# Matmul prices in a kernel's ordering model: from nominal values to the spacings of the trace

## Chip, cores, metric

The kernel runs on one core of one Trainium2 chip. The metric is the device time of one launch in microseconds (us); of three runs the median counts. A core has five engines that work side by side: PE (TensorE, matmuls), DVE (VectorE), ACT (ScalarE), POOL (GpSimd) and SP (SyncE, which here issues the DMAs). Each engine takes its instructions strictly in the order in which the program holds them, and waits at an instruction whose inputs are not there yet.

## What is computed

A sequence of 256 tokens of width 1024 goes through four layers, in fp32. Only what the text speaks of is shown:

```python
# layer 0, even: stick-breaking attention beside an S5 state-space mixer
h = rms_norm(x, even_norm_g[0]);  proj = h @ even_w_in[0]
q, k, v, z_a, u, z_b = split(proj)          # 1024 1024 1024 1024 512 512
q = rms_norm(q per head);  k = rms_norm(k per head)      # 8 heads of 128
o_a = stick_breaking_attention(q, k, v) * silu(z_a)
o_b = s5_mixer(u, ...) * silu(z_b)          # 32 groups, 64 complex states each
x = x + concat(o_a, o_b) @ even_w_out[0]
# layer 1, odd: gated linear attention, chunks of 64, 4 heads
q, k, v, z, r = split(rms_norm(x) @ odd_w_in[0])
log_a = log_sigmoid(r @ w_gate + b_gate) / 16
x = x + (rms_norm(gla(q, k, v, log_a)) * silu(z)) @ odd_w_out[0]
# layers 2 and 3, hybrid: dilated window attention beside retention
for l in range(2):
    h = rmsnorm(x) * (1 + scale) + shift    # from c @ w_ada
    y_att, y_ret = attention(h @ w_in), retention(h @ w_in)
    x = x + gate * ((sig(ga) * (y_att @ w_pa) + sig(gr) * (y_ret @ w_pr)) @ w_out)
return rmsnorm(x, final_norm_w)
# s5_mixer: lam_bar = exp(lam*dt); b_bar = (lam_bar-1)/lam * b
# state_t = lam_bar * state_(t-1) + b_bar u_t ; y = gelu(Re(c state) + d u); y * sigmoid(y @ w_glu + b)
```

## The kernel before

**The weights.** All large products are made of three fp32r matmuls. A weight tile of 128x2048 comes by DMA into `raw`; ACT copies it into `whi` (the high part, fp32r, 1024 columns at a time), DVE subtracts to make `wlo` (the low part, 512 columns at a time), and the product is whi·Hhi + whi·Hlo + wlo·Hhi, with H the normed activations, split alike. There are three slots each for `raw`, `whi` and `wlo`. `proj_a` writes tokens by 512 columns (PSUM tile `pa`, matmuls of 512 columns), `proj_b` writes 128 columns by 256 tokens (`pb`, 256 columns). `plan` fixes the order of the weight tiles: for the even layer q of the first four heads, u, k, v of the first half, q, k, v of the second half, then the gates and the output; then the odd and the hybrid layers.

**Beside the projections** the even layer has these steps, all named by their tiles. `qraw` is q or k of one half; its mean squares go through a chain of some ten small DVE steps (`rs`, Newton for 1/sqrt), DVE scales `qraw`, PE transposes it four heads at a time (`qtp`), and DVE writes qT or kT. There are four such sets: q and k of each half ("q0", "k0", "q1", "k1"). `stick_fiber` then makes the scores (`sbz`) of a half and its attention (`sb_sp`). The S5 mixer has one preparation on DVE (`s5_prep`: a long row of small steps, `s_w`, that ends in the table `s_W`, then a sign step on `s_W`, then `s_L` alike), and four blocks of states (0 to 3). In a block POOL makes the table `s5ez` from `s_W` (products into `s5ez` and `s5t`, then their sum), PE transposes it (`s5ep`), ACT copies it (`s5E`), PE multiplies with u (`s5vp`), ACT copies (`s5V`), PE rotates (`s5jp`), DVE combines (`s5B`, `s5m`, a scan over time, `s5V`), PE rotates again (`s5jp`), POOL and DVE multiply (`s5m`), and PE gives the block's output (`s5yp`), with POOL's `s5F`, `s5f` and PE's `s5gp`, `s5tp` as further tables. `s5ez`, `s5F`, `s5m`, `s5f` have one or few slots, so a block's tables wait for the block before. In the odd layer `la` (DVE) is the logarithm of the decay, PE sums it over time (`lgt`), and `gkt`, `gsc`, `gst` are the steps of the linear attention.

**What sets the order.** Nothing of the order is written by hand. Each layer is a set of generators ("fibers") that yield instructions; `Engine.make` gives each instruction a price (`i.cost`), and `run` keeps a clock for every engine: of all the fibers' next instructions it takes the one that could start first by these clocks (`when`, which adds a latency between engines; some fibers have a bias on it), emits it and advances its engine's clock by the price (`issue`). So the program of each engine is in the order in which the model thought that the instructions could start, and the prices of matmuls say how many projection matmuls the model puts on PE while another engine works at something. For a matmul with fp32r operands of n columns the price is 0.4167 n + 2.5 ns: 215.9 ns for the 512 columns of `pa`, 109.2 ns for the 256 of `pb`. Fp32 matmuls cost 1.667 n + 10 ns and at least 214 ns, a transpose 107 ns. Line 275 (`i.eng, i.emit = ...`) is the place where every instruction is recorded, so all rows of the trace carry L275, and the tiles' names tell them apart.

Of the kernel before, what the change touches and what calls it, by code (L numbers as in the profile page):

```python
# [8 lines left out]
F32 = mybir.dt.float32  # L9
# [7 lines left out]
P = 128  # L17
T = 256
# [9 lines left out]
# Newton's steps for a scaled 1/sqrt: s' = -2 s^3 takes the scale of the first guess to 32  # L28
# [6 lines left out]
# ---------------------------------------------------------------- weight order  # L35
def plan():
# [30 lines left out]
    # the ada tiles, spread between the others  # L67
# [26 lines left out]
# misc: 0:64 position numbers, 64:128 zero at position 0 and one after it  # L94
# [142 lines left out]
# ---------------------------------------------------------------- the program  # L237
# Each layer is written as fibers, generators of instructions. The instructions of all fibers are put in
# one order by a model of the engines: next comes the one that could start first.
# [21 lines left out]
class Engine:  # L261
    """Makes instructions; they are issued when their turn comes."""
# [4 lines left out]
    def __getattr__(self, op):  # L267
        real, name = getattr(self.real, op), self.name

        def make(*a, **k):  # L270
# [5 lines left out]
            # a tile of PSUM serves one engine at a time  # L276
# [11 lines left out]
            elif name == "pe":  # L288
                rhs = a[2] if len(a) > 2 else k["rhs"]
                if op == "transpose":  # L290
                    i.cost = 0.107
                else:
                    n = _cols(rhs)
                    i.cost = (0.4167 * n + 2.5) * 1e-3 if rhs.dtype == F32R else max(0.214, (1.667 * n + 10) * 1e-3)
# [19 lines left out]
class Prog:  # L314
    """What the layers share: engines, slots of memory, the weight stream, the fibers and their order."""
# [17 lines left out]
    # ---- fibers  # L333
# [12 lines left out]
    def stop(self, f, tl):  # L346
        """Ends a fiber and gives back its tile."""
        f["live"] = False
        self.fibers.remove(f)
        self.put(tl)  # L350
# [8 lines left out]
    def when(self, i):  # L359
        """When an instruction could start."""  # L360
# [72 lines left out]
    # ---- slots  # L433
# [42 lines left out]
    # ---- the weight stream: load, then the high and the low part of every tile  # L476
# [51 lines left out]
    def slack(self):  # L528
        """How far the weights are ahead of their use, in tiles."""
        return (self.made - self.used) / 2048.0  # L530
# [11 lines left out]
    # ---- shift, scale and gate: sums of weighted rows over the partitions' share, then over partitions  # L542
# [56 lines left out]
    # ---- projections  # L599
    def proj_a(self, h, blocks, steps, evac, ready=None, bias=0.0, halves=()):  # L600
        """Token-major [token, 512], activations stationary: blocks of keys; steps: (block, key, token tile).

        The blocks in halves come out as two halves, the first one early."""
# [27 lines left out]
    def proj_b(self, h, key, evac, nk=8, c0=0, last=True, ready=None):  # L631
        """Feature-major, two blocks of 128 features: weights stationary, 256 tokens move."""
# [17 lines left out]
    def copy_out(self, dst):  # L650
        """An evacuation by a copy."""
# [5 lines left out]
    # ---- small arithmetic  # L657
# [17 lines left out]
    def silu2(self, zp, g):  # L675
        """2 silu(z) of a PSUM tile, which is given back."""
# [5 lines left out]
    # ---- norm of the residual  # L682
    def square(self, tt, c, w=512, on_dve=False):
        """Adds the sum of squares of some columns to a token tile's."""
# [17 lines left out]
    def norm_rstd(self, tt):  # L702
        """1/sqrt of a token tile's mean square and EPS."""
# [14 lines left out]
    def norm(self, tt, scale, bias=None, flags=()):  # L718
        """The norm of a token tile, transposed, as high and low parts."""
# [67 lines left out]
    def h_end(self):  # L787
        """After a layer's last product with the norm."""
# [4 lines left out]
    def out_proj(self, mix, ready, blocks, nxt, res_gate=None, halves=()):  # L793
        """x += mix @ w_out. nxt(tt): the generator that goes on with a finished token tile."""
# [26 lines left out]
        # the first token tile is done as early as three tiles of weights let it  # L821
# [26 lines left out]
def program(g):  # L848
# [7 lines left out]
    # ---- loads  # L856
# [33 lines left out]
    # the tables of the first functions, and the array's clock, before the first data come  # L890
# [29 lines left out]
def reduce_angle(g, r, ang, k):  # L920
    """r = ang less the nearest multiple of two pi, within [-pi, pi]."""
# [24 lines left out]
def s5_prep(g, ev, S):  # L946
    """Tables of the S5 mixer that hang on its parameters alone."""
# [1043 lines left out]
```

## Time and profile before

| | |
|---|---|
| median of three runs | 1058.98 us (1058.54 to 1060.42) |
| profiled execution, its span | 1059.9 us |
| PE busy | 1031.7 us, 97% of the span, 7058 matmuls |
| DVE, ACT, POOL busy | 757.2, 502.3, 64.2 us |
| HBM | 189.31 MB read, 180 GB/s over the span |

The page gives the span of one execution and nothing around it. Busy time of PE includes the time in which several matmuls overlap in its pipeline, so the spacing of starts, not the length of one matmul, is what a matmul costs in a row of them; the chain of waits shows this spacing, since it lists a row of matmuls with its length from the first start to the last. The granted clock is the share of full TensorE speed that the chip allowed; its two levels are 1.0 (2.4 GHz) and 0.5 (1.2 GHz), and a stretch with a value between them had both.

### The profile page before, as it was taken

To read this page: it belongs to the slowest core of one execution; us is meant where nothing else is said; L and a number is where in the kernel's file an instruction comes from. 1 tells how busy PE (TensorE), PEld (TensorE's weight loads), DVE (VectorE), ACT (ScalarE), POOL (GpSimd) and SP (SyncE) were. 2 spreads that over 40 slices of the span, in tenths; PEclk is the share of its full clock that TensorE was granted. 3 is DMA by queue.
4 is the path that set the end of the run, shared out by engine and by line. 5 is a ranking of instruction groups with operands and counts; after the bars stand their busy time and mean duration, and the time that the engine had idled before them with its cause. 6 is when DMAs were issued, how large, how long until landed. Compare 5 with 4: busy or idle time off the path is not lost.

```text
span 1059.9 us, 17583 instructions
## 1 busy us (share of the span) xinstructions
PE 1031.7 (97%) x7058; PEld 948.3 (89%) x7058; DVE 757.2 (71%) x1607; ACT 502.3 (47%) x756; POOL 64.2 (6%) x79
## 2 busy tenths in 40 slices
PE   8989979999999999999999999999999999999997
PEld 7967769978899789999899999978999989999995
DVE  6996675968889776766588967674565658984565
ACT  6647427646634654434422443455453442343442
POOL 0146340000110000000000000000000000000000
PEclk9989899999999999999999999999999999999999
DMA  8641124463864658564444567445645444454541
GB/s 293 209 161 64 51 80 140 151 212 129 308 240 174 250 213 305 205 231 148 159 160 159 199 241 267 168 143 215 237 161 199 173 166 159 139 181 167 198 173 40
DMA packets 33501, 192.53 MB, mean 182 GB/s; under 512 B 8171, under 2 KB 9195, under 8 KB 11148
## 3 DMA queue, kind: packets, MB, share of 16 engines
q1 hardware_dynamic: 33132, 190.90, 50.6%
q8 instruction: 55, 0.90, 0.3%
q10 hardware_dynamic: 288, 0.52, 0.1%
q14 instruction: 26, 0.21, 0.1%
HBM read 189.31 MB, written 1.05 MB: 180 GB/s over the span
## 4 chain that ended last, share of the span: by engine, by line
PE 88%; DVE 8%; issue 1%; ACT 1%; DMA 1%; POOL 1%; SPq 0%; DVEq 0%; ACTq 0%
PE pb L275 52%; PE pa L275 21%; PE as L275 4%; DVE wlo L275 2%; PE ret L275 2%; DVE rs L275 2%; PE sbz L275 1%; DVE s_w L275 1%; PE s5yp L275 1%; PE ntp L275 1%; PE s5vp L275 1%; DMA cols<-in_cols_dram 1%; PE gsc L275 1%; PE qtp L275 1%; DVE s5B L275 1%
## 5 line engine op out<-in xcount | busy, mean ns | idle before, releaser
L275 DVE TENSOR_TENSOR wlo<-raw,whi 128x512 fp32r<-128x512 f32 x604 | 394.4, 693 | 166.0 <-ACT whi L275 161.2
L275 PE MATMUL pb<-H,whi 128*128 128x256 f32 x2688 | 494.6, 285 | 0.0
L275 ACT ACTIVATE whi<-raw 128x1024 fp32r<-128x1024 f32 x302 | 307.4, 1053 | 314.9 <-issue 161.6
L275 PEld LDWEIGHTS pb<-H,whi 128*128 128x128 f32 x2688 | 420.8, 192 | 3.0 <-issue 2.0
L275 PE MATMUL pb<-H,wlo 128*128 128x256 f32 x1344 | 382.6, 285 | 0.0
L275 PEld LDWEIGHTS pb<-H,wlo 128*128 128x128 f32 x1344 | 257.6, 192 | 0.5 <-issue 0.2
L275 PE MATMUL pa<-whi,H 128*128 128x512 f32 x576 | 187.4, 401 | 2.9 <-DVE H L275 2.9
L275 PEld LDWEIGHTS pa<-whi,H 128*128 128x128 f32 x576 | 109.2, 191 | 28.3 <-DVE H L275 5.2
L275 PE MATMUL pa<-wlo,H 128*128 128x512 f32 x288 | 114.7, 398 | 0.0
L275 PE MATMUL pb<-yy,whi 128*128 128x256 f32 x384 | 69.5, 283 | 0.0
L275 PEld LDWEIGHTS pa<-wlo,H 128*128 128x128 f32 x288 | 54.9, 191 | 11.3 <-issue 0.7
L275 DVE SCALAR_TENSOR_TENSOR acc<-raw,cact,acc 128x512 f32<-128x512 f32 x84 | 59.1, 745 | 4.4 <-DMA raw<-in_wall_dram 4.2
L275 PEld LDWEIGHTS pb<-yy,whi 128*128 128x128 f32 x384 | 59.9, 192 | 0.0
L275 PE MATMUL pb<-yy,wlo 128*128 128x256 f32 x192 | 54.3, 283 | 0.0
L275 PE MATMUL pa<-whi,mg 128*128 128x512 f32 (+1 forms) x144 | 41.1, 368 | 0.0
L275 PEld LDWEIGHTS pb<-yy,wlo 128*128 128x128 f32 x192 | 36.9, 192 | 0.0
L275 PEld LDWEIGHTS pa<-whi,mg 128*128 128x128 f32 x144 | 26.0, 188 | 5.1
L275 PE MATMUL pa<-whi,mix 128*128 128x512 f32 x96 | 30.2, 393 | 0.3 <-ACT mix L275 0.3
L275 DVE SCALAR_TENSOR_TENSOR rs<-rs 128x1 f32<-128x1 f32 (+3 forms) x144 | 28.5, 198 | 2.7
L275 DVE SCALAR_TENSOR_TENSOR tg<-tg,pb 128x512 f32<-128x512 f32 x16 | 11.0, 688 | 26.4 <-PE pb L275 26.4
L275 ACT ACTIVATE sqj<-x 128x512 f32<-128x512 f32 (+1 forms) x19 | 11.5, 608 | 35.7 <-DVE x L275 33.5
L275 PE MATMUL pa<-wlo,mg 128*128 128x512 f32 (+1 forms) x72 | 26.9, 374 | 0.0
(277 smaller groups left out, 1082.1 us busy)
## 6 DMA issues: line engine op xcount, KB each, us to landing
raw<-in_wall_dram SPq DMA_DIRECT2D x174, 1024.0 KB, 4.9
x<-in_x_dram SPq DMA_DIRECT2D x2, 512.0 KB, 5.9
raw<-in_wall_dram SPq DMA_DIRECT2D x2, 512.0 KB, 7.0
s5bc<-in_s5bc_dram SPq DMA_DIRECT2D x4, 256.0 KB, 2.5
gate<-in_bgate_dram SPq DMA_DIRECT2D x2, 512.0 KB, 5.6
c<-in_cst_dram SPq DMA_DIRECT2D x1, 896.0 KB, 7.1
cst<-in_cst_dram SPq DMA_DIRECT2D x1, 704.0 KB, 12.0
s_room<-s_room SPq DMA_DIRECT2D x16, 32.0 KB, 3.4
```

The lines of the kernel that those rows point to most:

```text
L275: i.eng, i.emit = name, (lambda: real(*a, **k))
```

## The change

The prices of PE's instructions are replaced by others: a transpose 112 ns for 107; an fp32r matmul 0.4167 n + 13.4 ns for 0.4167 n + 2.5 (512 columns: 226.8 for 215.9; 256 columns: 120.1 for 109.2); an fp32 matmul 1.667 n + 4 ns, at least 224, for 1.667 n + 10, at least 214. The prices of the other engines, the latencies and the biases stay. The other pieces of the diff take out comments and docstrings.

```diff
@@ -288,10 +288,10 @@
             elif name == "pe":
                 rhs = a[2] if len(a) > 2 else k["rhs"]
                 if op == "transpose":
-                    i.cost = 0.107
+                    i.cost = 0.112
                 else:
                     n = _cols(rhs)
-                    i.cost = (0.4167 * n + 2.5) * 1e-3 if rhs.dtype == F32R else max(0.214, (1.667 * n + 10) * 1e-3)
+                    i.cost = (0.4167 * n + 13.4) * 1e-3 if rhs.dtype == F32R else max(0.224, (1.667 * n + 4) * 1e-3)
             else:
```

The instructions are the same, in another order on every engine. Three places follow; a row is one instruction, or as many as its x says, with its tiles and its shape.

DVE, the end of the preparation of the S5 table `s_W`, before; `s_w` and `s_W` are its small steps, `wlo` the low parts of weights, `rs` the norm of k0:

```order
L275 TENSOR_TENSOR s_W<-s_w 128x32 x2
L275 TENSOR_TENSOR s_w<-s_W,s_w 128x32 x3
L275 TENSOR_TENSOR wlo<-raw,whi 128x512 x2
L275 TENSOR_TENSOR s_w<-s_W,s_w 128x32
L275 TENSOR_TENSOR wlo<-raw,whi 128x512 x2
L275 TENSOR_TENSOR s_W<-s_w 128x32
L275 TENSOR_TENSOR wlo<-raw,whi 128x512 x2
L275 TENSOR_TENSOR s_W<-s_w 128x32
L275 TENSOR_TENSOR s_w<-s_W,s_w 128x32
L275 TENSOR_SCALAR rs<-qss 128x8
```

The same place after, up to the sign step (the row with `sgc`) and the rows behind it:

```order
L275 TENSOR_TENSOR s_W<-s_w 128x32 x2
L275 TENSOR_TENSOR s_w<-s_W,s_w 128x32 x4
L275 TENSOR_TENSOR s_W<-s_w 128x32 x2
L275 TENSOR_TENSOR s_w<-s_W,s_w 128x32 x4
L275 TENSOR_TENSOR s_W<-s_w 128x32
L275 TENSOR_TENSOR wlo<-raw,whi 128x512
L275 TENSOR_TENSOR s_W<-s_w 128x32
L275 TENSOR_TENSOR wlo<-raw,whi 128x512
L275 TENSOR_SCALAR s_W<-s_W,sgc 128x128
L275 TENSOR_TENSOR wlo<-raw,whi 128x512 x2
L275 TENSOR_TENSOR s_w<-s_L,s_w 128x32
L275 TENSOR_TENSOR wlo<-raw,whi 128x512
```

Counted over the whole program up to the sign step, five `wlo` and five `rs` steps that stood ahead of it stand behind it now.

PE, from the transposes of block 0's table on, before; `qtp` are the transposes of k0:

```order
L275 MATMUL pa<-wlo,H 128x512
L275 MATMUL pa<-whi,H 128x512
L275 MATMUL s5ep<-cst_76,s5ez 128x128 x4
L275 MATMUL pa<-whi,H 128x512
L275 MATMUL pa<-wlo,H 128x512
L275 MATMUL pa<-whi,H 128x512
L275 MATMUL qtp<-cst_76,qraw 128x128 x4
L275 MATMUL pa<-whi,H 128x512
L275 MATMUL pa<-wlo,H 128x512
L275 MATMUL pa<-whi,H 128x512 x2
L275 MATMUL pa<-wlo,H 128x512
L275 MATMUL pa<-whi,H 128x512
```

And after:

```order
L275 MATMUL s5ep<-cst_76,s5ez 128x128 x4
L275 MATMUL pa<-whi,H 128x512
L275 MATMUL pa<-wlo,H 128x512
L275 MATMUL pa<-whi,H 128x512 x2
L275 MATMUL s5gp<-s5f_159,s5ez 128x32 x3
L275 MATMUL s5vp<-s_room,s5E 128x64 x8
L275 MATMUL s5gp<-s5f_159,s5ez 128x32
L275 MATMUL pa<-wlo,H 128x512
L275 MATMUL pa<-whi,H 128x512 x2
L275 MATMUL s5jp<-s5V,cst_103 128x512
L275 MATMUL s5tp<-s5f_159,cst_103 128x8x16 x3
L275 MATMUL s5tp<-s5f_159,cst_76 128x8x16
```

In after 213 projection matmuls stand ahead of this `s5ep`, in before 240, and k0's `qtp` comes 12 `pa` and most of block 0's PE steps behind it, where it came 3 `pa` behind. Projection matmuls ahead of the end of the blocks' `s5yp`: 273, 318, 347, 369 before (blocks 0 to 3), 239, 273, 309, 330 after. The `sbz` of the first half (12 products of qT and kT) stand before block 0's `s5yp` in before, behind it in after; the `qtp` of q1 ahead of and behind block 1's `s5yp` in before, behind block 2's in after; the `qtp` of k1 between block 3's `s5ep` and `s5vp` in before, 37 `pa` behind block 3's `s5yp` in after.

POOL, around the end of block 0, before (`s5F` is block 0's table, the rows from `s5f` on are block 1's, except `s5m`, which is block 0's):

```order
L275 TENSOR_TENSOR s5F<-s5F,s5t 128x512
L275 MEMSET s5B 128x8
L275 TENSOR_SCALAR s5f_920<-s5bc,sgc 128x128
L275 TENSOR_TENSOR s5ez<-s_W,s5bc 128x16x16 x2
L275 TENSOR_TENSOR s5t<-s_W,s5bc 128x16x16 x2
L275 TENSOR_TENSOR s5m<-s_room,s5B 128x512
L275 TENSOR_TENSOR s5ez<-s5ez,s5t 128x512
```

And after:

```order
L275 MEMSET s5B 128x8
L275 TENSOR_TENSOR s5F<-s5F,s5t 128x512
L275 TENSOR_TENSOR s5m<-s_room,s5B 128x512
L275 TENSOR_SCALAR s5f_820<-s5bc,sgc 128x128
L275 TENSOR_TENSOR s5ez<-s_W,s5bc 128x16x16 x2
L275 TENSOR_TENSOR s5t<-s_W,s5bc 128x16x16 x2
L275 TENSOR_TENSOR s5ez<-s5ez,s5t 128x512
```

Block 0's `s5m` now stands ahead of block 1's tables. On SP a few loads of weight tiles change places with those of the S5 tables and with copies of the S5 output. In the odd layer `lgt` stands 20 `pb` earlier on PE; in the hybrid layers the steps beside the projections move by at most eight or so projection matmuls, and the ends of the layers move by eight matmuls at most.

## Rows read from the trace of the kernel before

**Rows 1.** the page: busy time by engine; granted clock in 40 slices.
```profile
PE 1031.7 (97%) x7058; PEld 948.3 (89%) x7058; DVE 757.2 (71%) x1607; ACT 502.3 (47%) x756; POOL 64.2 (6%) x79
...
PEclk9989899999999999999999999999999999999999
```

**Rows 2.** windows: length, busy PE PEld DVE ACT POOL, granted clock, DMA, GB/s.
```profile
50.00:100.00 50.00, 44.20 (x231) 35.28 (x230) 41.40 (x116) 31.30 (x56) 24.05 (x25) 0.90 0.39 128
100.00:150.00 50.00, 42.72 (x240) 34.07 (x239) 35.70 (x62) 22.41 (x55) 25.15 (x29) 0.90 0.19 63
...
450.00:500.00 50.00, 50.00 (x398) 48.96 (x397) 30.38 (x61) 21.72 (x33) 0.00 (x0) 1.00 0.57 204
...
700.00:750.00 50.00, 48.26 (x244) 39.74 (x243) 32.21 (x71) 30.58 (x48) 0.00 (x0) 1.00 0.51 176
```

**Rows 3.** chain of waits, 490 to 530: start, length, what.
```profile
498.98 21.79 PE pa L275 x96
```

**Rows 4.** the same view, 945 to the end.
```profile
950.74 78.71 PE pb L275 x656
```

**Rows 5.** PE in order of time: start, length, what, [idle before, its releaser].
```profile
62.46 0.66 PE L275 MATMUL s5ep<-cst,s5ez 128*128 128x128 f32 x4 [0.99 <-POOL s5ez L275]
...
67.45 1.09 PE L275 MATMUL qtp<-cst,qraw 128*128 128x128 f32 x4 [3.63 <-DVE qraw L275]
...
87.14 0.41 PE L275 MATMUL s5yp<-s_room,s5T 128*128 128x64 f32 x2 [1.13 <-DVE s5m L275]
...
115.02 0.66 PE L275 MATMUL qtp<-cst,qraw 128*128 128x128 f32 x4 [1.89 <-DVE qraw L275]
...
137.02 0.41 PE L275 MATMUL s5yp<-s_room,s5T 128*128 128x64 f32 x2 [1.87 <-DVE s5m L275]
...
144.18 1.11 PE L275 MATMUL qtp<-cst,qraw 128*128 128x128 f32 x4 [3.27 <-DVE qraw L275]
```

**Rows 6.** windows, the stretch around the longest of those waits.
```profile
65.30:72.10 6.80, 4.65 (x15) 3.97 (x16) 5.89 (x10) 0.00 (x0) 6.72 (x5) 0.50 0.52 164
```

**Rows 7.** windows from s5ep of block 0 on, cut behind each block's s5yp.
```profile
62.46:89.87 27.41, 22.60 (x129) 17.96 (x129) 21.71 (x45) 14.32 (x27) 16.57 (x15) 0.86 0.35 125
89.87:120.12 30.25, 28.36 (x151) 22.18 (x150) 21.46 (x43) 20.05 (x44) 11.60 (x14) 0.89 0.23 79
120.12:139.50 19.38, 17.26 (x99) 13.63 (x97) 13.04 (x18) 8.29 (x18) 13.50 (x14) 0.92 0.16 47
139.50:159.16 19.66, 16.17 (x99) 12.75 (x95) 13.12 (x22) 3.44 (x6) 5.44 (x7) 0.91 0.22 76
```

**Rows 8.** DVE in order of time.
```profile
52.72 1.29 DVE L275 TENSOR_TENSOR wlo<-raw,whi 128x512 fp32r<-128x512 f32 x2
...
55.34 1.29 DVE L275 TENSOR_TENSOR wlo<-raw,whi 128x512 fp32r<-128x512 f32 x2
...
58.30 0.64 DVE L275 TENSOR_TENSOR rs<-rs 128x8 f32<-128x8 f32 x1
58.86 0.72 DVE L275 TENSOR_SCALAR s_W<-s_W,sgc 128x128 f32<-128x128 f32 x1
...
66.63 1.28 DVE L275 TENSOR_TENSOR qraw<-qraw,rs 128x512 f32<-128x512 f32 x2
```

**Rows 9.** POOL in order of time.
```profile
59.73 1.31 POOL L275 TENSOR_TENSOR s5t<-s_W,s5bc 128x256 f32<-128x256 f32 x2 [0.23 <-DVE s_W L275]
61.12 1.28 POOL L275 TENSOR_TENSOR s5ez<-s5ez,s5t 128x512 f32<-128x512 f32 x1
...
131.95 2.09 POOL L275 TENSOR_TENSOR s5t<-s_W,s5bc 128x256 f32<-128x256 f32 x2
...
135.69 1.72 POOL L275 TENSOR_TENSOR s5ez<-s5ez,s5t 128x512 f32<-128x512 f32 x1
```

**Rows 10.** tile lgt: count, durations min/median/max, first and last start.
```profile
L275 PE MATMUL lgt<-cst,la x16: 270/275/275, 284.2 to 285.8; 128*128 128x128 f32 x16
...
L275 DVE SCALAR_TENSOR_TENSOR la<-lgt,la x1: 1217/1217/1217, 281.8 to 281.8; 128x1024 f32<-128x1024 f32 x1
```

## The prediction

> **What bounds the kernel now.** I read first the page's busy times, then the windows of 50 us, then the chain of waits, and last PE's own row of instructions where the windows show holes. PE is busy for 1031.7 of 1059.9 us, and the granted clock is full but for a few slices of the first sixth [rows 1]. The windows say where the rest is: from 450 to 500 us PE has no hole at all and the full clock, from 700 to 750 it lacks 1.74 us, but from 50 to 100 it lacks 5.80 us and from 100 to 150 7.28 us, both at a mean clock of 0.90 [rows 2]. So the kernel is bound by the stream of matmuls nearly everywhere, and by the small chains of DVE, POOL and ACT in the even layer, where PE runs out of things that it may do. A reordering takes no matmul away; it can win only holes and half-clock time, and nearly all of these lie between 50 and 160 us.
>
> The chain also shows what a matmul costs in a row: 96 `pa` in 21.79 us, 227 ns each [rows 3], and 656 `pb` in 78.71 us, 120 ns each [rows 4]. The new prices (226.8 and 120.1) are these; the old ones (215.9 and 109.2) were 5 and 9% too low, so the model believed PE early with its projections and put more of them ahead of a step than there was time for. The order of before therefore had some cover built in by mistake: a PE that arrives later than the model thinks. What happens when that goes is the question.
>
> Of the holes, six hold 12.8 us [rows 5]: 0.99 us at block 0's `s5ep` (POOL's `s5ez`), 3.63 at k0's transposes, 1.13 at block 0's `s5yp`, 1.89 at q1's transposes, 1.87 at block 2's `s5yp`, 3.27 at k1's transposes. The clock falls with them: around the longest the grant is 0.50, the lower level of 1.2 GHz, for 6.8 us [rows 6]. I cut the stretch behind each block's `s5yp` [rows 7] and split its loss into holes (length less PE busy) and clock ((1 - mean grant) x length, which is what half-speed time costs if PE had work all along):
> - block 0, 27.41 us: holes 4.81, clock 3.84
> - block 1, 30.25 us: holes 1.89, clock 3.33
> - block 2, 19.38 us: holes 2.12, clock 1.55
> - block 3, 19.66 us: holes 3.49, clock 1.77
>
> Together 22.8 us: the ceiling of what the order could win here.
>
> **The change part by part.** I hold each step of the new order against the point at which it would cost nothing: its old time, less the PE work that now stands behind it instead of ahead.
>
> *Block 0's start.* 27 projection matmuls fewer stand ahead of `s5ep`: 27 x 0.227 = 6.13 us, so it breaks even at 62.46 - 6.13 = 56.33. It waits for POOL's `s5ez`, and that for the sign step on `s_W`, which ended at 58.86 + 0.72 = 59.58 [rows 8]; POOL then needed until 61.12 + 1.28 = 62.40, 2.82 us [rows 9]. Five `wlo` less ahead of the sign step save 5 x 0.65 = 3.2 us (1.29 for two), and of the five `rs` steps the one at 58.30 alone 0.56 to the next start [rows 8]; the other four are too short to count. The sign step then ends at 55.8, `s5ez` at 58.6, and `s5ep` starts near 58.65: **+2.3 us** against break-even. The low end is 0, if DVE comes to the sign step another 2.3 us earlier than counted; the high end comes from company. In before only small steps ran on DVE while POOL made this table, in after the `wlo` that were pushed back. Where DVE was dense with `wlo` (block 3's table), the same two POOL steps took 2.09 and 1.72 us instead of 1.31 and 1.28 [rows 9]: 1.2 us more, so +3.5.
>
> The Trainium skill speaks against the change here: "SBUF — State Buffer", section "SBUF: two separate sides", says that DVE and GpSimd share a port pair as an exclusive lock, that a DVE step with two SBUF inputs contends with a GpSimd step that reads SBUF, and that the loser waits for the whole instruction. `wlo` has two SBUF inputs. The rows of block 3 agree with it (2.09 against 1.31); by this rule the high end would be the likely one.
>
> *Block 0 to its `s5yp`.* The hole at k0's transposes does not go. Behind the sign step DVE now has six `wlo` ahead of `qraw` instead of two (+2.6 us), the five `rs` steps and some five steps of S5 (about 0.65 each, as a `wlo`, an estimate: 3.3). It took 66.63 - 59.58 = 7.05 us before [rows 8]; about 13.5 now, from 55.8 to 69.3, and 0.8 for the first half of the scaling, as before (66.63 to 67.45) [rows 5, 8]: 70.1. PE is there at 58.65 + 12 x 0.227 + the S5 steps (about 4.9, an estimate from the lengths that PE spent on them) = 66.3. The hole is 3.8, as before 3.63. What goes is the 1.13 at `s5yp`: block 0's `s5m` stood behind three of POOL's steps for block 1's tables, now ahead of them. **-1.1 us**, with 0 and -8.6 (all of the block's loss) as ends; I stay near 0 because the large hole stays, and the half clock with it.
>
> *Block 1.* q1's transposes move from around block 1's `s5yp` to behind block 2's, some 9.8 us of PE work later, so the hole of 1.89 is not on the way any more; half of the slow clock (1.7) goes with it, the other half belongs to the holes of block 0. **-3.6 us** (0 to -5.2).
>
> *Block 2.* The wait of `s5yp` for `s5m` stays: the number of projection matmuls between is about the same (21 between `s5jp` steps and `s5yp`, before and after), and DVE now has q1's `rs` steps among its own. Half of the clock's loss goes with block 1's hole: **-0.8 us** (+1.5, eight `rs` steps of about 0.2 us more ahead of `s5m`, to -3.7).
>
> *Block 3.* k1's transposes, whose hole was the 3.27, move behind `s5yp` and 37 further `pa` (8.4 us of cover, where DVE still has some 8 `wlo`, 5 us, and the `rs` chain to do); half of the clock's loss goes with it: 3.27 + 0.9 = **-4.2 us** (0, if the hole appears at the new place, to -5.3). The work that moved behind block 3's `s5yp` (39 `pa` and eight transposes, 39 x 0.227 + about 0.9 = 9.7 us) is covered there: behind it PE has only projections.
>
> *The odd layer.* The second row of `lgt` started at 284.2, 1.2 us after `la` ended at 281.8 + 1.217 = 283.0 [rows 10]. It stands 20 `pb` earlier, 20 x 0.120 = 2.4 us, and DVE's share does not move by itself: 2.4 - 1.2 = **+1.2 us**, up to +3 if the following steps (`gkt`, `gsc`, 2 us earlier too) wait again, 0 if DVE's `wlo` ahead of `la` are fewer.
>
> *The rest.* In the hybrid layers the steps move by a microsecond of PE work or less, where PE now has no hole [rows 2]; the holes at the ends of the layers (1.74 us around 708) have the same chain before and after. 0 (-1 to +2). The DMAs move on SP, but HBM is at 180 GB/s, and POOL's and SP's other rows are not late anywhere that PE waits. 0.
>
> Sum: 2.3 - 1.1 - 3.6 - 0.8 - 4.2 + 1.2 = **-6.2 us**. On the profiled execution's 1059.9 that is 1053.7. This execution lies 0.9 us above the median of the runs, so on the scale of the runs 1052.8. I say **1053**.
>
> **The rivals.**
>
> *The holes only change place.* A chain of DVE, POOL and ACT that lasts as long as before makes PE wait for it somewhere: what q1's transposes no longer wait, `s5yp` waits a little later, since each block's products wait for the same `s5m`. For this speaks that all six holes end with DVE or POOL and that these two have the same work to do; against it that PE's work between the blocks is unchanged while DVE is dense only in parts. Then only k1's 4.2 us are real: 2.3 + 1.2 - 4.2 = -0.7, **1058**, no difference that a measurement of this kernel could tell (about 0.2%, 2.1 us).
>
> *Slower: the lost cover.* The too low prices gave each S5 step of PE more projections ahead than the model counted, and these hid the chains' real latencies. In after PE comes 6.1 us earlier to block 0's table and 9.7 us earlier to block 3's output than to the same steps in before, the chains do not get shorter, and POOL and DVE meet at the `wlo` that were pushed back. With no hole won back in blocks 0 to 3, the table late by the 1.2 us of company, and the odd layer as above: 2.3 + 1.2 + 1.2 = +4.7, and another 1.5 where block 2's `s5m` waits behind `rs`: **1064 to 1065**. It decides from where less than 4.7 of the 22.8 us, a fifth, is won back. The rule of the port pair belongs to this case.
>
> *Faster by much.* Two thirds of the blocks' loss goes: -15 + 3.5 = -11.5, **1047**. The holes and the half clock hang together, so one that vanishes takes 1 to 3 us of slow clock along.
>
> That the order does not change is out: the programs differ on every engine.
>
> **How the numbers follow.** The forecast (1049 to 1057) has 0.42, much faster (below 1049) 0.16, holes moved (1057 to 1061) 0.22, lost cover (above 1061) 0.20. The range of 8 in 10 runs from 1046.5 to 1062.5. Faster by over 0.2% (below 1056.9) is the first two, 0.58; within 0.2% 0.21; slower 0.21.
>
> **What would show it.** In the profile of after: `s5ep` of block 0 near 58.6 with a wait of some 2 to 3 us for `s5ez`; the wait at k0's transposes still above 3 us; none at q1's and k1's; block 3's `s5yp` over near 142 instead of 159.2, where 159.16 - 9.7 = 149.4 is break-even; `lgt` with a wait of about 1 us. If the mean clock from 50 to 150 us is still 0.90, blocks 1 and 3 are wrong. The prediction is wrong as a whole if the windows behind 400 us show holes that are not there now, since I priced them at nothing, or if `s5yp` of block 1 or 2 waits for over 3 us.

## The result

The change makes the kernel slower: 1069.75 us (median of four runs, 1068.53 to 1072.16) against 1058.76 us, a ratio of 1.0112 with a 95% interval of 1.0094 to 1.013: 11 us where 6 us of gain were forecast, and above the range. The profiled execution has a span of 1067.5 us.

The page of after, busy time and granted clock, against [rows 1]:

```profile
PE 1038.0 (97%) x7055; PEld 951.9 (89%) x7055; DVE 764.8 (72%) x1607; ACT 500.8 (47%) x755; POOL 67.8 (6%) x79
...
PEclk9988999999999999999999999999999999999999
```

PE's busy time has grown by 6.3 us, though the trace holds three matmuls fewer: the model fills the start of the program with warm-up matmuls whose result nobody reads, and at the higher price it puts 31 of them there instead of 34. ACT has one table load (ACT_TABLE_LOAD) fewer, 9 for 10. All other instructions are the same. The clock dips in the third and fourth of the 40 slices, where before it dipped in the third and fifth. The windows (length, busy PE, PEld, DVE, ACT, POOL, granted clock, DMA share, GB/s), against [rows 2]:

```profile
50.00:100.00 50.00, 42.58 (x206) 34.11 (x204) 46.26 (x104) 28.70 (x49) 30.66 (x31) 0.83 0.30 97
100.00:150.00 50.00, 45.70 (x259) 35.83 (x259) 31.92 (x50) 20.57 (x50) 24.17 (x25) 0.93 0.20 69
...
300.00:350.00 50.00, 48.79 (x347) 45.79 (x346) 43.48 (x94) 23.29 (x40) 1.69 (x3) 1.00 0.62 223
...
400.00:450.00 50.00, 49.28 (x386) 47.35 (x384) 36.09 (x69) 22.24 (x32) 0.00 (x0) 1.00 0.68 241
```

Between 50 and 100 us PE lacks 7.42 us instead of 5.80, at a clock of 0.83 instead of 0.90; between 100 and 150 it lacks 4.30 instead of 7.28, at 0.93 instead of 0.90; and there is something new, small holes far behind: 1.21 us between 300 and 350, 0.72 between 400 and 450. What PE waited for, all of it in microseconds, times, the longest:

```profile
PE s5yp L275 <- DVE s5m L275: 4.1, 2, 3.6
...
PE s5ep L275 <- POOL s5ez L275: 2.5, 1, 2.5
PE s5jp L275 <- DVE s5V L275: 2.3, 3, 1.5
...
PE s5vp L275 <- ACT s5E L275: 1.6, 1, 1.6
PE pa L275 <- DVE wlo L275: 1.6, 3, 0.6
...
PE gst L275 <- ACT kc L275: 1.0, 1, 1.0
PE gate_p L275 <- issue: 0.7, 1, 0.7
```

The three waits for `qraw`, together 8.8 us of before [rows 5], are gone. In their place stand longer waits at `s5ep`, `s5vp`, `s5jp`, `s5yp` and for the weights (`wlo`): the holes have changed place. There are more of them, but in sum they have not grown: from the first projection to the last one of the even layer's input the listed waits come to 13.3 us in before and 12.5 in after. What has grown there is the time at half clock. The blocks of after, cut as [rows 7]:

```profile
58.98:80.44 21.46, 20.51 (x98) 16.21 (x98) 21.20 (x50) 8.29 (x13) 13.83 (x15) 0.76 0.29 100
80.44:112.01 31.57, 28.48 (x160) 23.68 (x158) 22.15 (x30) 21.22 (x39) 15.75 (x15) 0.89 0.22 75
112.01:133.89 21.88, 18.17 (x104) 14.01 (x101) 17.51 (x29) 8.17 (x18) 13.72 (x14) 0.94 0.24 78
133.89:150.65 16.76, 16.38 (x95) 13.12 (x94) 8.76 (x13) 6.48 (x16) 5.46 (x7) 0.87 0.10 42
```

The stretches at the lower level sum to 20.4 us in before, PE busy for 17.9 of them, and to 23.9 us in after, PE busy in all of it. Half of the difference in busy time, 3.0 us, is lost to the clock.

**Where the time went.** A row of matmuls gives a clean measure of progress: in both programs the same projections stand in each layer, so I take from PE's order of time the starts of the last projection of a layer's input, of its output, and so on, and count them from the first projection (15.26 us in before, 13.07 in after: the first projection comes up to 2 us sooner or later from execution to execution, in rest_new at 13.57 with the order of before). The table gives the loss of each stage against the profiled execution of before:

| stage | after | even_new | rest_new | rest_lat | mm_only | lat_up | mm_mid | mm_eps | mm_high | mm_low |
|---|---|---|---|---|---|---|---|---|---|---|
| even layer, input projections | +4.4 | +6.5 | -2.2 | -3.7 | +2.9 | +3.4 | +1.6 | +7.4 | +5.4 | -5.8 |
| even layer, output | -0.7 | -0.7 | 0.0 | 0.0 | -0.7 | -0.9 | -0.9 | 0.0 | -0.7 | +10.6 |
| odd layer | +2.4 | 0.0 | +1.9 | +2.1 | +2.2 | +0.7 | +1.1 | +0.3 | +9.2 | +9.6 |
| first hybrid layer | +2.4 | 0.0 | +1.6 | +0.5 | +2.5 | +1.1 | +0.3 | 0.0 | +9.1 | -1.3 |
| second hybrid layer | +1.2 | 0.0 | +1.2 | 0.0 | +1.2 | -0.1 | +0.2 | +0.1 | +3.0 | +0.3 |

rest_new and rest_lat have the even layer of before, instruction for instruction, and yet their profiled executions went through it 2.2 and 3.7 us faster: the even layer, with its holes and its half clock, varies by some 3 us between executions, and before's profile was a long one. Part of it is the clock alone: from 100 to 150 us rest_new was granted 0.97 where before had 0.90. The time of before's profiled execution says so as well: the execution with the span of 1067.5 us took 1069.26, so the span of 1059.9 stands for some 1061.7, 3 us above the median. So the first line of the table is only good to about 3 us, and the timed ratios decide there; the lines of the later layers repeat to within 0.8 us in the three kernels that have the new fp32r price there (after, rest_new, mm_only).

### The profile page after: what moved, and what is told of

It reads as the page before. It is cut to its first block, busy times and chain, and to the rows that moved or that the text cites. A ratio compares the mean times of both kernels' runs of the same rounds, so it can differ in the third digit from the quotient of the medians.

```text
span 1067.5 us, 17588 instructions
## 1 busy us (share of the span) xinstructions
PE 1038.0 (97%) x7055; PEld 951.9 (89%) x7055; DVE 764.8 (72%) x1607; ACT 500.8 (47%) x755; POOL 67.8 (6%) x79
## 4 chain that ended last, share of the span: by engine, by line
PE 65%; DVE 4%; ACT 1%; issue 1%; DVEq 0%; ACTq 0%
PE pb L275 44%; PE pa L275 14%; PE as L275 4%; PE ret L275 2%; DVE wlo L275 1%; DVE rs L275 1%; ACT nf L275 0%; PE gate_p L275 0%; DVE H L275 0%; PE rtp L275 0%; DVE gzo L275 0%; PE ntp L275 0%; PE gsc L275 0%; DVE acc L275 0%; PE at L275 0%
## 5 line engine op out<-in xcount | busy, mean ns | idle before, releaser
L275 DVE SCALAR_TENSOR_TENSOR acc<-raw,cact,acc 128x512 f32<-128x512 f32 x84 | 58.7, 745 | 10.6 <-DMA raw<-in_wall_dram 10.6
```

The source lines that it names most:

```text
L275: i.eng, i.emit = name, (lambda: real(*a, **k))
```

## The experiments

Two theories were tested. **Cover**: the low prices of before made the model put more projections ahead of each dependent step than it thought, and that hid what the model lacks; with the true prices each layer loses its share. **Scatter**: any other price draws another order, and orders differ by several microseconds without a trend. A third, **company**, came from block 0's table: POOL and DVE meet there. In all kernels the instructions are the same but for the warm-up matmuls and that one table load, only their order differs. Prices that change at the end of the even layer are made so:

```diff
-                    i.cost = 0.112
+                    i.cost = PRICE[0]
...
+PRICE = [...]
...
+            PRICE[:] = [0.112, 13.4, 0.224, 4]
             yield from even_layer(g, ev)
+            PRICE[:] = [0.107, 2.5, 0.214, 10]
```

**even_new and rest_new: which layers lose.** The diff above is even_new; rest_new has the two rows the other way round.

> The new prices while the even layer is ordered, the old ones from the odd layer on. Theory C (cover: the too low prices put more projections ahead of each step than the model thought, and that hid latencies that the model lacks; each layer loses its share): about +4 us, since the milestones of the two traces, counted from the first projection, differ by +4.4 us at the end of the even layer's projections and +3.8 at the end of its output. Theory P (POOL and DVE meet at the S5 tables, the rest is a consequence): the whole loss, +9 to +11. Theory S (any change of prices draws another order, and orders scatter by several us): +4 here, as the even layer is that of the changed kernel.

> The old prices while the even layer is ordered, the new ones from the odd layer on. Theory C: +5 to +6 us (the milestones: +2.4 in the odd layer, +2.4 and +1.2 in the hybrid layers). Theory P: within 2 us of before. Theory S: anything from -3 to +6, since the odd layer starts from another state of the model's clocks.

even_new took 1063.73 us, 1.0058 of before (1.0041 to 1.0074); rest_new 1063.44 us, 1.0054 (1.0038 to 1.007). The losses of the halves, 5.9 and 5.6 us against before's 1057.86, add up to the whole, 11. Company as the cause of everything is out: half of the loss arises in layers where POOL has next to nothing to do.

**mm_low and mm_high: the direction.** Only the fp32r price, one step down and two steps up:

```diff
-                    i.cost = (0.4167 * n + 2.5) * 1e-3 if rhs.dtype == F32R else max(0.214, (1.667 * n + 10) * 1e-3)
+                    i.cost = (0.4167 * n - 8.4) * 1e-3 if rhs.dtype == F32R else max(0.214, (1.667 * n + 10) * 1e-3)
```

This is mm_low; mm_high has + 24.3 in that place.

> Only the price of the fp32r matmuls is changed, and the other way: 0.4167 n - 8.4 ns instead of + 2.5, the same step of 10.9 ns down that the change went up; transposes and fp32 matmuls at the old prices. Theory C: more cover still, so no wait of PE that before does not have: -4 to +2 us, and the waits at s5ep and s5yp gone; what it can cost is an evacuation that comes late. Theory S: another draw, within +-8 us, as likely slower as not.

> Only the price of the fp32r matmuls is changed, by twice the step: 0.4167 n + 24.3 ns, which is above the spacings of the trace. Theory C: PE comes to every step earlier still, +18 to +25 us. Theory S: within +-8 us of before, with no trend from 2.5 over 13.4 to 24.3.

mm_high took 1087.05 us, 1.0281 (1.0264 to 1.0298): +29 us, in the direction of cover, above its 18 to 25, and far beyond the 8 us of scatter. By the table 21 us of it arise behind the even layer; the even layer loses about as much as in after, although the price is moved twice as far. PE's waits behind 246 us, the longest (before has only waits for `H` there, 2.9 us):

```profile
PE ada_p L275 <- DVE acc L275: 3.1, 4, 1.1
PE ntp L275 <- DVE xn L275: 2.6, 5, 0.8
PE gate_p L275 <- ACT whi L275: 2.1, 1, 2.1
```

But mm_low took 1074.49 us, 1.0162 (1.0142 to 1.0183), where cover expected no loss and scatter at most 8 us. Up to the end of the even layer's input it is 5.8 us ahead; then it loses 10.6 us at the layer's output and 9.6 in the odd layer. What PE waited for there:

```profile
PE pb L275 <- ACT mix L275: 7.9, 1, 7.9
PE ada_p L275 <- DVE acc L275: 5.4, 1, 5.4
```

and the chain that ended last, at the end of the even layer (start, length, what):

```profile
168.83 25.69 PE pb L275 x213
...
207.24 0.35 DVE mix L275
```

Block 3's `s5yp` was over at 168.8, where the first row starts, some 10 us later than before. Behind it stand only 213 `pb`; when they are done, the S5 output still has to go through `y`, `gz` and `mix` on DVE, and PE has no projections left while it waits for `mix`. So cover has an end: a projection that is put ahead of a step of S5 delays S5, and the layer's output needs S5. So the price can lose on either side, by holes of PE when it is high and by a late end of the chain when it is low. Why `acc` came 5.4 us late in the odd layer was not followed.

**mm_mid and mm_eps: the size.**

The same line with + 8.0 in mm_mid and + 3.0 in mm_eps.

> The old prices but for 0.4167 n + 3.0 ns instead of + 2.5 for the fp32r matmuls, a twentieth of the change. The order of the even layer moves by a matmul or two. Theory C: +0.5 us, not to be told from before. Theory S: if orders scatter whatever the size of the step, +-4 us.

> The old prices but for 0.4167 n + 8.0 ns for the fp32r matmuls, half of the change. Theory C, with before near the best point between too much ahead (a step that ends the layer comes late) and too little (PE waits): +4 to +7 us, half of the changed kernel's loss. Theory S: within +-8 us of before, not between the two.

Half of the change costs nothing that the runs can tell (1058.74 us, 1.0013, 0.9996 to 1.003); a twentieth of it costs 9 us (1067.38 us, 1.0092, 1.0064 to 1.0119). mm_eps loses all of it in the even layer. Up to block 0's `s5ep` its order is that of before to within a matmul or two, but the first half's attention (`sbz` from `sb_sp`) has come to stand behind block 1's steps, where PE waits for DVE's `sb_sp`, and block 0's `s5yp` waits longer. PE in order of time (start, length, what, idle before and its releaser):

```profile
88.72 0.41 PE L275 MATMUL s5yp<-s_room,s5T 128*128 128x64 f32 x2 [2.94 <-DVE s5m L275]
...
114.45 2.07 PE L275 MATMUL sbz<-sb_sp,cst 128*128 128x512 f32 x2 [4.20 <-DVE sb_sp L275]
```

4.20 us at one row that did not wait in before. Half-clock time goes with it: the granted clock of its four runs was 0.981 to 0.988, and the run with 0.981 took 1069.46 us, the one with 0.988 took 1063.12. In the even layer scatter holds in kind; in size it was put too low, at 4 us.

**even_20, even_50, even_80: scatter in the even layer alone.** The prices as in even_new's diff, with 2.0, 5.0 and 8.0 for 13.4 and the old ones for the rest.

> The fp32r price of 0.4167 n + 2.0 ns while the even layer is ordered, the old prices behind it: half a nanosecond down, as mm_eps was half a nanosecond up, where the even layer lost 7.4 us by the milestones. Theory S for the even layer (its time does not follow the price, but how a few steps fall): anything from -6 to +8; its order puts block 3's s5yp behind 414 projection matmuls instead of 369, so I say slower, +2 to +8, as the S5 chain ends late. Theory C: within 0.5 us of before.

> The fp32r price of 0.4167 n + 5.0 ns while the even layer is ordered, the old prices behind it. Theory C: +1 us. Theory S: anything from -6 to +8, whatever lies on either side of it (mm_eps with 3.0 is 9 us slower than before, mm_mid with 8.0 is not); its blocks follow each other with 31, 26 and 28 projection matmuls between their s5yp, where before has 45, 29 and 22, and no transposes stand ahead of block 3's s5yp: I say -3 to +1.

> The fp32r price of 0.4167 n + 8.0 ns while the even layer is ordered, the old prices behind it. mm_mid, with 8.0 everywhere, was 0.5 us above before, and by its milestones lost 1.6 behind the even layer. Theory S for the even layer: the same even layer as mm_mid's and no loss behind, -2 to +1 against before. If the even layer follows the price: +3.

| fp32r price in the even layer, 0.4167 n + | 2.0 | 2.5 | 3.0 (mm_eps) | 5.0 | 8.0 | 13.4 (even_new) |
|---|---|---|---|---|---|---|
| ratio to before | 1.0063 | 1 | 1.0092 | 1.0008 | 1.0006 | 1.0058 |
| interval | 1.0043 to 1.0083 | | 1.0064 to 1.0119 | 0.9991 to 1.0025 | 0.9988 to 1.0023 | 1.0041 to 1.0074 |

There is no trend. even_20 loses 6.8 us by the stages at the output of the even layer, as mm_low does: its block 3 comes late. None of the draws is measurably faster than before, which is among the good ones.

**pool_up, comp, no_comp: company.** pool_up raises POOL's price to what its steps took beside DVE; comp keeps the old prices and moves five `wlo` behind the sign step, as the change does; no_comp keeps the new prices in the even layer and moves most of them away again:

```diff
-                                     else 2.1e-3) * n + 0.48 * cols
+                                     else 3.2e-3) * n + 0.48 * cols
```

This is pool_up. In comp the fiber that makes `wlo` (`lows`) is held; "cm" is set at the first multiplication of `s_W`, "s5W" at the sign step:

```diff
+                if "cm" in self.flags and "s5W" not in self.flags:
+                    yield lambda: not ("cm" in self.flags and "s5W" not in self.flags)
                 (hi, low), raw = self.tiles[key], self.raws[key]
```

no_comp is even_new with the same two lines for "s5W" and "ez0", which is set when block 0's `s5ez` is issued.

> The changed kernel, and in its model POOL's price of a two-input step raised from 2.1 to 3.2 ns a column (1.69 us for 512 columns, what such steps took in the trace of the changed kernel beside DVE: 1.69 to 1.72). It puts six more projection matmuls ahead of block 0's s5ep. Theory P: the waits at s5ep and s5yp shrink, -3 to -6 us against the changed kernel, all of it in the even layer. Theory C: -1 to -2 (s5ep's 2.5 us wait only, the others come from DVE's and ACT's chains). Theory S: within 8 us either way.

> The old prices everywhere; only the low parts of weights are held back on DVE from the first multiplication of the s_W table until its sign step is issued, so that five wlo stand behind the sign step, as in the changed kernel. The model answers with 223 projections ahead of block 0's s5ep and 247, 280, 309, 332 ahead of the ends of the blocks' s5yp, nearly the row of the changed kernel (213; 239, 273, 309, 330; before 240; 273, 318, 347, 369). If this swap is the cause of the even layer's loss: s5ez takes 6 us instead of 4, and +4 to +7 in all. If the prices act by many small moves: 0 to +2.

> As even_new (new prices in the even layer, old ones behind), but wlo are held back on DVE from the sign step on s_W until the last POOL step of block 0's s5ez is issued. One wlo stays directly behind the sign step, four come behind twelve small steps. If the meeting of wlo and POOL is the cause: s5ez near 4.5 us, and -2 to -3 against even_new, +3 to +4 to before. If not: another draw, within +-6 of even_new.

Company is there. POOL's steps for block 0's table started in before with this row and ended at 62.40 [rows 9], 4.10 us later:

```profile
58.30 1.21 POOL L275 TENSOR_TENSOR s5ez<-s_W,s5bc 128x256 f32<-128x256 f32 x2 [16.48 <-DVE rs L275]
```

In after they took 6.08 us:

```profile
52.84 2.26 POOL L275 TENSOR_TENSOR s5ez<-s_W,s5bc 128x256 f32<-128x256 f32 x2 [12.81 <-DVE s_W L275]
55.06 2.09 POOL L275 TENSOR_TENSOR s5t<-s_W,s5bc 128x256 f32<-128x256 f32 x2
57.23 1.69 POOL L275 TENSOR_TENSOR s5ez<-s5ez,s5t 128x512 f32<-128x512 f32 x1
```

and 5.17 in comp (53.19 to 58.36), where the moved `wlo` stand in the same place: about half of the 2 us. It does not set the time by itself. comp, with the swap and with nearly the row of steps of the changed kernel on PE, is at 1059.37 us, 1.0016 (1.0002 to 1.0031), though its waits are not fewer: 7.6 us at `s5yp` in three places, and these two:

```profile
55.21 0.50 PE L276 MATMUL pa<-wlo,H 128*128 128x512 f32 x1 [2.33 <-DVE wlo L276]
...
66.88 0.49 PE L276 MATMUL s5tp<-s5f,cst 128*128 128x128 f32 x2 [3.47 <-DVE s5f L276]
```

no_comp shortened the table only to 5.30 us (54.20 to 59.50; 4.5 was expected) and stayed at 1.0077 (1.0053 to 1.0102); neither that nor comp changes company by more than about half, so company as a part of the loss is not ruled out. pool_up cut the wait at `s5ep` from 2.5 to 0.8 us and stayed at 1069.66 us, 1.012 (1.01 to 1.0141), neither theory's gain: PE now waited 5.29 us at k0's transposes, for DVE's `qraw`, where after has no wait. And even_80, which loses nothing, still has these holes:

```profile
62.86 0.66 PE L276 MATMUL s5ep<-cst,s5ez 128*128 128x128 f32 x4 [1.63 <-POOL s5ez L276]
...
70.38 1.12 PE L276 MATMUL qtp<-cst,qraw 128*128 128x128 f32 x4 [3.51 <-DVE qraw L276]
```

So neither the swap nor the wait at `s5ep` makes the loss of the even layer by itself.

**lat_up, rest_lat, mm_only: cover in the later layers.** lat_up is the changed kernel with 0.15 us more in the model before a matmul that reads another engine's result; rest_lat is rest_new with the same from the odd layer on; mm_only has only the fp32r price.

```diff
-                        t = max(t, e + LAT[g])
+                        t = max(t, e + LAT[g] + (0.15 if i.eng == "pe" else 0))
```

> The changed kernel, and in its model 0.15 us more between the end of an instruction of another engine and a matmul that reads from it: one or two projection matmuls more ahead of every dependent step of PE, put there on purpose. Theory C: the small waits of the odd and the hybrid layers (ret on rat, as, gst, gate_p) go, so that from the end of the even layer on it loses 0 to 1.5 us to before where the changed kernel loses 6; the even layer stays at +3 to +6, as its waits are longer than 0.15: +3 to +7 in all. Theory S: no relation, within 8 us of the changed kernel.

> As rest_new (old prices in the even layer, new ones from the odd layer on), but from the odd layer on the model also counts 0.15 us more before a matmul that reads another engine's result. The matmuls' prices are those of rest_new, only the cover is given back. Theory C for the late layers: the +5.6 us of rest_new shrink to 0 to +2. If the late layers lose for another reason (the true prices themselves, or scatter), +4 or more.

> Of the change only the fp32r price (0.4167 n + 13.4 ns), with the old prices for transposes and fp32 matmuls. If the loss of the late layers is lost cover, it is there with this price alone, since the cover consists of pa and pb: +5 to +6 us from the end of the even layer on. The even layer: another draw, 0 to +8.

rest_lat took 1059.66 us, 1.0023 (1.001 to 1.0035): of rest_new's 5.6 us some 2.1 are left, with the same true prices of matmuls. By the stages the hybrid layers lose 0.5 us instead of 2.8, the odd layer 2.1, about the 1.9 of rest_new. PE's waits behind 246 us, first of rest_new, then of rest_lat:

```profile
PE pa L276 <- DVE H L276: 2.1, 3, 1.1
PE ntp L276 <- DVE xn L276: 1.5, 5, 0.4
PE ada_p L276 <- DVE acc L276: 1.0, 2, 0.5
```

```profile
PE pa L276 <- DVE H L276: 2.3, 3, 1.1
PE gst L276 <- ACT kc L276: 1.4, 1, 1.4
PE ntp L276 <- DVE xn L276: 1.0, 3, 0.4
```

The waits of `ada_p` are gone and those of `ntp` shorter; the one new wait, `gst` for `kc`, is in the odd layer, where the rest of the loss is. lat_up took 1068.29 us, 1.0117 (1.0091 to 1.0143), so there is no gain as a whole, where cover expected +3 to +7 us against before; behind the even layer its profile loses 1.7 us where after's loses 6.0, with 0.7 in the odd layer. That its even layer is another bad draw is an inference: the profiled run is the fastest of its four (1063.56 us, clock 0.990; the others 1067.51 to 1071.88, clock 0.984 or 0.985), and of the others there is no profile. mm_only took 1068.82 us, 1.0102 (1.0087 to 1.0117), with +5.9 us behind the even layer: the loss comes from the prices of `pa` and `pb`, of which the cover consists; those of transposes and fp32 matmuls make no difference that these runs can tell (1.0112 with them, 1.0094 to 1.013).

## Why the prediction was wrong

PE's spacing and the place of the holes were read rightly, and but for three warm-up matmuls and one table load no instruction changes. The scale was not: I put the profiled execution 0.9 us above the median by its span, and it was some 3 us above it, so some 2 us of what I saw as loss may be missing in most runs. The forecast failed in the even layer's blocks 1 and 2, in the half clock that was to go with the holes, and in the layers that I priced at nothing. PE in order of time, after, up to block 1 (the row at 80.44 is the first behind block 0's `s5yp`):

```profile
13.07 0.39 PE L275 MATMUL pa<-whi,H 128*128 128x512 f32 x1
...
58.98 0.66 PE L275 MATMUL s5ep<-cst,s5ez 128*128 128x128 f32 x4 [2.54 <-POOL s5ez L275]
...
80.44 0.80 PE L275 MATMUL pa<-whi,H 128*128 128x512 f32 x1
...
88.96 1.22 PE L275 MATMUL s5vp<-s_room,s5E 128*128 128x64 f32 x9 [1.63 <-ACT s5E L275]
...
100.20 1.10 PE L275 MATMUL s5jp<-s5V,cst 128*128 128x512 f32 x2 [1.46 <-DVE s5V L275]
```

and at block 2 (133.89 is the first row behind its `s5yp`) and behind block 3:

```profile
130.45 0.41 PE L275 MATMUL s5yp<-s_room,s5T 128*128 128x64 f32 x2 [3.64 <-DVE s5m L275]
...
133.89 1.12 PE L275 MATMUL qtp<-cst,qraw 128*128 128x128 f32 x4
...
150.65 0.50 PE L275 MATMUL pa<-whi,H 128*128 128x512 f32 x1
```

Counted from the first projection, as in the table, these rows and the break-even points (the old end [rows 7] less the PE work that has moved behind it: 10.4, 10.7, 9.5 and 9.7 us for blocks 0 to 3) give the loss of each term:

- **Block 0's start, forecast +2.3, measured +4.8** (58.98 - 13.07 = 45.9; break-even 56.33 - 15.26 = 41.1). The mechanism was right, the size was not: the wait for `s5ez` is there (2.54 us), and `s5ep` starts when `s5ez` is done. The sign step on `s_W` is this row of DVE:

```profile
53.95 0.65 DVE L275 TENSOR_SCALAR s_W<-s_W,sgc 128x128 f32<-128x128 f32 x1
```

It ended 41.5 us behind the first projection, where the forecast has 55.8 - 15.26 = 40.5, so it came 1.0 us later than forecast; from there POOL took 4.3 us (54.60 to 58.92) instead of 2.82, 1.5 more, where the high end had 1.2. PE's three waits for `wlo` (1.6 us) lie ahead of this wait and add nothing to it. The waits of PE between 20 us and this row rise with the price: 0 in mm_low, 0.9 to 1.6 us from 2.0 to 8.0, 4.3 in after.
- **Block 0, forecast -1.1, measured -1.6** (67.4 against 64.2, +3.2 in sum). The size was about right by luck: I kept the large hole at k0's transposes, and there is none. The block's holes fell from 4.81 to 0.95 us, but the clock took more than before: from 59.79 to 70.02, right behind the wait for `s5ez`, the grant was 0.50 while PE was busy without a hole, and the block's mean fell from 0.86 to 0.76.
- **Block 1, forecast -3.6, measured +1.6** (its last `s5yp` row ended at 112.1, 99.0 against 94.2, +4.8 in sum). The step that failed is "the hole is not on the way any more". q1's transposes did move away, but PE then waited at `s5vp` for ACT's `s5E` (1.63 us) and at `s5jp` for `s5V` (1.46 us): together they are the block's 3.09 us of holes (1.89 before). The chain lasts, and PE waits at another step of it. This is the rival that the holes only change place.
- **Block 2, forecast -0.8, measured +1.3** (120.8 against 114.7, +6.1). The wait for `s5m` did not stay at 1.87, it became 3.64. I had priced q1's eight `rs` steps between `s5V` and `s5m` at 0.2 us each; DVE in order of time shows otherwise:

```profile
123.27 0.68 DVE L275 TENSOR_TENSOR s5V<-s_room,s5B 128x512 f32<-128x512 f32 x1
...
126.08 1.80 DVE L275 SCALAR_TENSOR_TENSOR rs<-rs 128x8 f32<-128x8 f32 x2
127.92 1.19 DVE L275 TENSOR_TENSOR rs<-rs 128x8 f32<-128x8 f32 x1
...
129.63 0.68 DVE L275 TENSOR_TENSOR s5m<-s5jp,s5m 128x512 f32<-128x512 f32 x1
...
131.34 0.17 DVE L275 TENSOR_TENSOR rs<-rs 128x8 f32<-128x8 f32 x1
```

The steps of 128x8 elements at 126.08 and 127.92 take 0.9 to 1.2 us each, while POOL works beside them on block 2's `s5m` and block 3's table (126.61 to 129.09). At 131.34, when POOL is idle, such a step takes 0.17.

- **Block 3, forecast -4.2, measured -2.7** (137.6 against 134.2, +3.4). Right for the hole: no wait at k1's transposes any more, and 0.38 us of holes instead of 3.49. The half clock did not go with it (0.87, before 0.91).
- **The half clock of blocks 1 to 3, forecast -3.4 of the terms above (1.7, 0.8, 0.9).** It did not come: by the formula of the forecast blocks 0 to 3 lost 12.1 us to the clock in after and 10.5 in before, although their holes fell from 12.3 to 8.1 us. Ahead of block 0 the holes rose from 1.0 to 4.3 us, and right behind these came the longest stretch at half clock, 10.2 us. So the half clock was wrongly booked out block by block, with each block's own hole. How much of this belongs to the order is not settled, since the clock differs between executions of one order, as rest_new shows.
- **The odd layer, forecast +1.2, measured +2.4.** The wait came, but not at `lgt`; it is at `gst`, for ACT's `kc`:

```profile
310.20 1.99 PE L275 MATMUL gst<-vO,kc 128*128 128x256 f32 x8 [1.00 <-ACT kc L275]
```

It is 1.0 of the 2.4 us; the list of waits does not show the rest.

- **The rest, forecast 0, measured +3.6.** This is the gravest error: I took "PE has no hole here" for "there is room". The margins were thin; steps that stand a few `pb` earlier met them. One of them, in the first hybrid layer, is a wait for nothing that the profile shows:

```profile
421.38 1.10 PE L275 MATMUL gate_p<-acc,cst 128*128 128x512 f32 x2 [0.72 <-issue]
```

Others are too short for a list of waits: in both hybrid layers the 56 passes of `ret` take 10.04 us from start to start instead of 9.43.

The rival of lost cover had the right sign and was given 0.20; it had 1064 to 1065 because it, too, left out the hybrid layers. Both signs that the forecast had named for being wrong as a whole came: `s5yp` of block 2 waits for over 3 us, and behind 400 us there are holes that before does not have.

**What is settled and what is not.** Shown: half of the loss is in the even layer, half behind it. In the hybrid layers it is lost cover: the loss behind the even layer follows the price from 2.5 over 8.0 and 13.4 to 24.3 (0, 1.6, 6.0 and 21 us), and in the hybrid layers it goes when the model's latency gives the cover back. In the odd layer cover is not shown to be the cause: 2.1 us stay in rest_lat, 0.7 in lat_up, and this was not tried further. Shown too: in the even layer the time does not follow the price, and the one swap on DVE does not make it. Open: which of the many moves in blocks 0 to 3 makes 13.4 a bad draw there and 5.0 and 8.0 good ones, and how much of it is half-clock time that the order brings on; only the waits ahead of block 0's `s5ep` are common to after, even_new, mm_only and lat_up, all with 13.4 (3.6 to 4.3 us; 1.0 in before).

## To carry to other kernels

In a kernel whose order comes from a model, a single price that is made true is not an improvement by itself: the other numbers were chosen beside the wrong one, and a price that is too low can stand for a latency that is missing. If a price is corrected, put the cover back on purpose, where a step waits, and time the parts of the program one by one; a stretch without holes is not a stretch with room. And where a small serial chain decides the order, try a few neighbouring values before believing any of them, since half a nanosecond in a price moved this kernel by 9 us.

## What the runs showed of the hardware

A small step on DVE can last about as long as the POOL step beside it. In before such a step of 128x32 elements ran alone (POOL's first table began at 58.30):

```profile
53.92 0.20 DVE L275 TENSOR_TENSOR s_w<-s_W,s_w 128x32 f32<-128x32 f32 x1
```

In after, beside POOL's first table:

```profile
56.60 0.60 DVE L275 TENSOR_TENSOR s_w<-s_L,s_w 128x32 f32<-128x32 f32 x1
...
57.72 1.25 DVE L275 TENSOR_TENSOR s_w<-s_L,s_w 128x32 f32<-128x32 f32 x1
```

The same kind of step took 0.20 us alone and up to 1.25 us in company. Both of these ended within 0.1 us of a POOL step (57.20 against 57.15, 58.97 against 58.92).

POOL is slowed too (6.08 us for 4.10). The Trainium skill, "SBUF — State Buffer", section "SBUF: two separate sides", has the rule, a lock on a shared port pair that is held for a whole instruction. The trace agrees with it by these ends. The high end that I set beside this rule in the forecast (1.2 us) counted only POOL's last two steps, and for these it was right (2.09 and 1.69 us). It left out the first products into `s5ez`, which took 2.26 us instead of 1.21, with `wlo` beside them too.
